# Late Q and K loads in rows of 2 KB, and one late store cut by partitions, in a cross-covariance attention kernel

## The chip, the cores and the metric

The kernel runs on one core of a Trainium2 chip. The metric is the device time of one execution in microseconds; of several executions the median is taken.

## The reference

Q, K and V have the shape (8, 12, 512, 64) in float32: 96 heads, 512 rows, 64 columns. Attention is taken between columns, not rows:

```python
Q_norm = Q / (norm(Q, axis=-2) + 1e-10)          # each column of 512 rows
K_norm = K / (norm(K, axis=-2) + 1e-10)
attn = einsum('bhnd,bhne->bhde', Q_norm, K_norm)  # 64 x 64 a head
attn = softmax(attn, axis=-1)
return einsum('bhnd,bhde->bhne', V, attn)
```

Q, K and V are 12.6 MB each, and so is the output: 50.3 MB have to pass between DRAM and the core.

## The kernel before, in words

The heads are taken four at a time: a **unit** u, 24 of them (`U`). Two units make a **step** s with halves r = 0 and 1 (u = 2s + r; 12 steps, `S`), and two steps share one V tile pair w (6 of them). In DRAM the units lie in the order w, r, e, where s = 2w + e.

For a unit, Q and K are loaded by `load_qk` with 16 rows of a head on a partition: 32 partitions a head, 4 KB in one piece for each partition. `cast_qk` writes them beside each other as bf16 (DVE). `grams` multiplies [Q K] by itself on TensorE, 32 partitions at a time: 16 products for each of four heads, 64 products a unit, each one a weight load and a matmul. The diagonal of the result gives the norms (`squares`, `sums`, `powers`), one quarter is Q times K (`cross`), which is scaled (`scale_k`), transposed (`logits`), exponentiated (`exps`) and normalised (`normalise`). V is loaded in rows of 8 KB (`load_v`), cast (`cast_v`, POOL or DVE), transposed on TensorE (`vtrans`, copied by `vcopy`), multiplied by the attention (`outs`, line 318), copied to the tile `so` (`ocopy`, ACT or DVE), and stored by `store`, two stores of 512 KB a step, 24 in all, with 2 KB in one piece.

All loads but two leave from SP's queue (the two first K loads leave from ACT), and so do all stores. The trace shows eight DMA semaphores in turn for this queue: a DMA is issued when the one eight places ahead has landed on all engines. In what follows this is called a lane.

The order of everything is made ahead of time by the class `Order`: each step of work is a piece with costs, what it must wait for, and a rank; a planner runs through them and emits the instructions in the order of its own times. Loads have the rank `QK_PACE * u / U` (lines 382 to 390) and `v_at`, stores that of V later by `ST_LAG`. `size` tells the planner how many TensorE instructions a piece has, because the planner models the fetching of TensorE's instructions in chunks of 256 (`pause`).

Some names that the change touches: `WIDE` is the first unit whose Q and K are loaded in another shape, with 8 rows of a head on a partition (64 partitions a head, two pieces of 2 KB for each partition, `Qw` and `Kw`), whose grams then take 64 partitions and 8 products a head. Before, `WIDE` is `U`, so no unit is of that kind. `parts(s)` says which steps load their two units by separate DMAs of 512 KB; the others load both by one DMA of 1 MB. `FEW = (S - 3, 1)` is one late store, the second of step 9; before, it leaves in four parts: partitions 0 to 91, 92 to 95 and 96 to 127 of its first half r = 0, and all 128 of its second half.

Of the kernel before, what the change touches and what calls it, by code (L numbers as in the profile page):

```python
# [102 lines left out]
def kernel(  # L103
# [7 lines left out]
    nc = tc.nc  # L111
    B, H, N, _ = Q.shape
    assert N == 32 * T and Q.shape[3] == D
    U = B * H // HU
    S = U // 2
    W = S // 2
    TAIL = 2
    WIDE = U
    ONE = 3
    HELD, UNTIL = ("lk", 1, 1), ("cq", 0, 1)  # L120
    BOTH = S - 8
# [10 lines left out]
    Qw = Q.rearrange("b h (p j) d -> (b h p j d)", j=J).rearrange("(u m p x) -> u p m x", m=2, p=128, x=J * D)  # L132
    Kw = K.rearrange("b h (p j) d -> (b h p j d)", j=J).rearrange("(u m p x) -> u p m x", m=2, p=128, x=J * D)
# [28 lines left out]
    qk32, v32, vb, qkb, gram, scr, kq, n2, r8, kqs, rq, lg, ex, ab, vps, vt, po, so = ({} for _ in range(18))  # L162
# [9 lines left out]
    def load_qk(s, x, r):  # L172

        w, e = divmod(s, 2)
        if s not in qk32:
            qk32[s] = qp.tile([128, 2, 2, T, D], F32, name="qk32")
        if HELD == ("l" + "qk"[x], s, r):

            nc.vector.memset(qk32[s][0:1, x, r, 0, 0:1], 0.0)
        if (s, x) == (0, 1):  # L180
            nc.scalar.dma_start(out=qk32[s][:, x, r].rearrange("p t d -> p (t d)"), in_=Ku[w, e, :, r])
        elif 2 * s + (r or 0) >= WIDE:
            nc.sync.dma_start(out=qk32[s][:, x, r].rearrange("p (m j) d -> p m (j d)", m=2), in_=(Qw, Kw)[x][U - 1])
        elif r is None:
            nc.sync.dma_start(out=qk32[s][:, x].rearrange("p r t d -> p r (t d)"), in_=(Qu, Ku)[x][w, e])  # L185
        else:
            nc.sync.dma_start(out=qk32[s][:, x, r].rearrange("p t d -> p (t d)"), in_=(Qu, Ku)[x][w, e, :, r])
# [10 lines left out]
    def store(s, i):  # L198
        o = Of[s // 2, s % 2, i].rearrange("p r (j d) -> p r j d", d=D)
        if (s, i) == FEW:  # L200

            for a, b in ((0, 92), (92, 96), (96, 128)):
                nc.sync.dma_start(out=o[a:b, 0], in_=so[s, i][a:b, 0])
            nc.sync.dma_start(out=o[:, 1], in_=so[s, i][:, 1])
            return
        nc.sync.dma_start(out=o, in_=so[s, i])

# [12 lines left out]
    def grams(u):  # L220
# [3 lines left out]
        if r == 0:  # L224
            gram[s] = ps_g.tile([128, HU, 2, 2, 2 * D], F32, name="gram")
        for t in range(T if u < WIDE else J):
            for h in range(HU):
                if u < WIDE:
                    x = qkb[u][32 * h:32 * (h + 1), t, :]
                else:  # L230
                    x = qkb[u][64 * (h % 2):64 * (h % 2 + 1), J * (h // 2) + t, :]
                nc.tensor.matmul(gram[s][:, h, r, 0], x, x, start=(t == 0), stop=(t == (T if u < WIDE else J) - 1))  # L232

# [96 lines left out]
    for r in range(2):  # L330
        load_qk(0, 0, r)
        load_qk(0, 1, r)
# [14 lines left out]
    for i in range(NB["ab"]):  # L347
        a = const.tile([128, HU, 2 * D], BF16, name=f"ab{i}")
# [3 lines left out]
    def size(key):  # L352
        if key[0] == "gr" and key[1] >= WIDE:
            return 64
        return 8 if key[0] == "vt" and key[-1] is not None else {"gr": 128, "lg": 8, "vt": 16, "ou": 16}[key[0]]
# [18 lines left out]


    def parts(s):
        return (0, 1) if s < ONE or s == S - 1 else (None,)

    def loaded(x, s, r):
        return ("l" + "qk"[x], s, r if len(parts(s)) == 2 else None)  # L380

    last = None
    for s in range(S):
        free = [back("cq", 2 * s + r, 2 * NB["qk"], x) for r in range(2) for x in range(2)]
        for r in parts(s):
            at = QK_PACE * (2 * s + (r or 0)) / U
            for x in range(2):
                key = loaded(x, s, r)
                piece(key, {"DMA": X if r is not None else 2 * X}, free, [last], at, load_qk, s, x, r)
                last = key  # L390
    for u in range(U):
        s, r = divmod(u, 2)
# [48 lines left out]
    for s in range(S):  # L441
        for x in range(4):
            i, k = divmod(x, 2)
            n = 4 * s + x - 2
            wait = [("oc", n // 4, n % 4)] if n >= 0 else []
            order = [("ou", s, x - 1) if x else back("ou", s, 1, 3)]
            piece(("ou", s, x), {"PE": 0.5}, [("vc", s // 2, *t) for t in turns(s // 2) if t[0] // 2 == k] + [("nm", s)] + wait, order, R["ou"] + 0.01 * s, outs, s, x)
            n = 2 * s + i - NB["so"]
            free = [("st", n // 2, n % 2)] if k == 0 and n >= 0 else []
            order = [("oc", s, x - 1) if x else back("oc", s, 1, 3)]  # L450
            piece(("oc", s, x), {"ACT": 0.6, "DVE": (0.68, BIAS["oc"])} if s >= BOTH else {"ACT": 0.6}, [("ou", s, x)] + free, order, R["oc"] + 0.01 * s, ocopy, s, x)
        for i in range(2):
            order = [("st", s, 0) if i else back("st", s, 1, 1)]
            piece(("st", s, i), {"DMA": X}, [("oc", s, 2 * i), ("oc", s, 2 * i + 1)], order, v_at(2 * s + i) + ST_LAG, store, s, i)
# [43 lines left out]
```

## Time and profile before

| | |
|---|---|
| median of 3 runs | 129.41 us (129.15 to 129.7) |
| span of the profiled execution | 127.4 us, 4949 instructions |
| profiled execution's own time | given as its span alone; the median lies 2.0 us above it |
| PE, PEld, DVE, ACT, POOL busy | 77.0, 62.7, 92.9, 72.3, 37.0 us |
| PE instructions | 2160 matmuls and 2160 weight loads |
| DMA | 14958 packets, 50.66 MB, mean 398 GB/s |
| queue of SP (q1) | 14648 packets, 95.9% of 16 engines' span |
| queue q8, kind instruction | 17 packets, 0.28 MB, 0.8% |
| HBM | 395 GB/s over the span |

The span runs from the first to the last instruction of the profiled execution. The row of DMA digits on the page gives for 40 equal slices how busy the 16 DMA engines were on average, in tenths. Times below are counted from the start of the span. A **lag** in the text is how much later one of the 16 DMA engines finishes its share of a DMA than the foremost engine does; it is read from the landing events that the trace keeps for each DMA, one for each engine that took part.

### The profile page before, as it was taken

Reading aid. Unit: us, or ns where it says so; the run is one execution under the profiler, and the core shown is the slowest. Engines: PE = TensorE matmul, PEld = TensorE weight load, DVE = VectorE, ACT = ScalarE, POOL = GpSimd, SP = SyncE. Lnnn points to the kernel's source line nnn. Section 1 sums busy time; section 2 is a strip of 40 time slices with the busy share of each in tenths; the row PEclk is TensorE's granted clock in tenths of the full one; section 3 lists DMA queues with packets and bytes.
Section 4 is the critical chain, followed back from the end, with each engine's and each line's share of the span. In section 5 each row is a group of like instructions: output and inputs, shape, how many; then the busy total and the mean of one; then the engine's idle time right before and its main releaser. Section 6 shows DMA issues by size and latency. Waiting matters only on the chain.

```text
span 127.4 us, 4949 instructions
## 1 busy us (share of the span) xinstructions
PE 77.0 (60%) x2160; PEld 62.7 (49%) x2160; DVE 92.9 (73%) x142; ACT 72.3 (57%) x220; POOL 37.0 (29%) x39
## 2 busy tenths in 40 slices
PE   0065393994837679859475986777597729753000
PEld 0054372783636568647354674666386517541000
DVE  3344749949899899999974989998999499950000
ACT  4000441559877077886691897583848919996000
POOL 4006307300916903033077011303733160300000
PEclk9999999999985555999996799869959995999755
DMA  4999999999999999999999999999999999999991
GB/s 113 413 438 408 428 411 418 417 433 408 435 418 414 411 417 424 402 415 427 423 414 414 415 428 417 415 424 425 401 420 419 401 402 410 395 408 408 375 377 60
DMA packets 14958, 50.66 MB, mean 398 GB/s; under 512 B 1112, under 2 KB 1112, under 8 KB 13400
## 3 DMA queue, kind: packets, MB, share of 16 engines
q1 hardware_dynamic: 14648, 49.29, 95.9%
q10 hardware_dynamic: 288, 1.05, 2.1%
q8 instruction: 17, 0.28, 0.8%
q14 instruction: 5, 0.04, 0.1%
HBM read 37.75 MB, written 12.58 MB: 395 GB/s over the span
## 4 chain that ended last, share of the span: by engine, by line
DVE 36%; PE 21%; DMA 19%; issue 8%; ACT 5%; SPq 1%; DVEq 0%; ACTq 0%
DVE qkb L212 15%; DMA qk<-in_K_dram 14%; PE gram L232 12%; DVE scr L239 7%; DMA qk<-in_Q_dram 5%; DVE vt L168 4%; PE vps L301 4%; DVE ab L290 4%; PE po L318 3%; ACT so L166 3%; DVE n L251 2%; ACT ex L281 2%; DVE vb L168 2%; PE lg L275 1%; SPq L185 1%
## 5 line engine op out<-in xcount | busy, mean ns | idle before, releaser
L232 PE MATMUL gram<-qkb 32*128 32x128 bf16 x1536 | 36.7, 259 | 24.8 <-issue 8.5
L232 PEld LDWEIGHTS <-qkb 32*128 32x128 bf16 x1536 | 30.8, 116 | 29.7 <-issue 11.1
L212 DVE CAST qkb<-qk 128x1024 bf16<-128x1024 f32 x48 | 37.7, 810 | 9.6 <-DMA qk<-in_Q_dram 8.0
L170 POOL TENSOR_SCALAR vb<-v 128x1024 bf16<-128x1024 f32 x18 | 21.7, 1215 | 43.9 <-DMA v<-in_V_dram 39.0
L166 ACT COPY vt<-vps 128x1024 bf16<-128x1024 bf16 (+1 forms) x18 | 17.8, 986 | 18.8 <-PE vps L301 18.7
L166 ACT COPY so<-po 128x512 f32<-128x512 f32 x45 | 24.9, 593 | 6.1 <-PE po L318 5.8
L318 PE MATMUL po<-ab,vt 128*64 128x128 bf16 x384 | 19.1, 237 | 6.2 <-issue 2.6
L262 POOL TENSOR_TENSOR kqs<-kq,r 64x512 f32<-64x512 f32 x12 | 14.0, 1169 | 29.1 <-ACT r L258 16.2
L301 PE MATMUL vps<-identb,vb 128*128 128x128 bf16 x192 | 18.5, 253 | 4.8 <-POOL vb L170 3.5
L239 DVE SCALAR_TENSOR_TENSOR scr<-gram,eye 64x512 f32<-64x512 f32 x24 | 16.5, 687 | 4.9 <-PE gram L232 4.7
L318 PEld LDWEIGHTS <-vt 128*64 128x64 bf16 x384 | 13.4, 117 | 10.4 <-issue 5.7
L301 PEld LDWEIGHTS <-vb 128*128 128x128 bf16 x192 | 14.0, 113 | 7.9 <-POOL vb L170 4.2
L281 ACT ACTIVATE ex<-lg,rq 128x64 f32<-128x64 f32 x48 | 14.5, 322 | 2.7 <-PE lg L275 2.6
L166 ACT COPY kq<-gram 64x512 f32<-64x512 f32 x12 | 7.0, 582 | 13.2 <-DVE scr L239 12.9
L290 DVE TENSOR_TENSOR ab<-ex,rinv 64x256 bf16<-64x256 f32 x24 | 12.8, 534 | 0.6
L281 ACT ACTIVATION_READ_ACCUMULATOR ex<-lg,rq 128x1 f32 x48 | 10.2, 213 | 0.0
L168 DVE CAST vb<-v 128x1024 bf16<-128x1024 f32 x6 | 7.4, 1241 | 1.8 <-DMA v<-in_V_dram 1.7
L275 PE MATMUL lg<-eye,kqs 64*128 64x64 f32 x48 | 6.4, 259 | 3.2 <-issue 1.6
L251 DVE TENSOR_REDUCE n<-scr 128x8 f32<-128x512 f32 x12 | 8.1, 679 | 0.1
L168 DVE COPY vt<-vps 128x1024 bf16<-128x1024 bf16 (+1 forms) x8 | 8.0, 1022 | 0.2
L275 PEld LDWEIGHTS lg<-eye,kqs 64*128 64x128 f32 x48 | 4.5, 156 | 5.0 <-issue 2.5
L287 DVE RECIPROCAL rinv<-esum 128x4 f32<-128x4 f32 x12 | 2.0, 170 | 2.5 <-ACT ex L281 2.4
(17 smaller groups left out, 16.0 us busy)
## 6 DMA issues: line engine op xcount, KB each, us to landing
v<-in_V_dram SPq DMA_DIRECT2D x12, 1024.0 KB, 17.4
out_dram<-so SPq DMA_DIRECT2D x23, 512.0 KB, 11.2
qk<-in_Q_dram SPq DMA_DIRECT2D x8, 1024.0 KB, 16.8
qk<-in_K_dram SPq DMA_DIRECT2D x8, 1024.0 KB, 18.8
qk<-in_Q_dram SPq DMA_DIRECT2D x8, 512.0 KB, 11.9
qk<-in_K_dram SPq DMA_DIRECT2D x6, 512.0 KB, 12.6
qk<-in_K_dram ACTq DMA_DIRECT2D x2, 512.0 KB, 7.3
out_dram<-so SPq DMA_DIRECT2D x1, 256.0 KB, 7.2
```

The source lines that it names most:

```text
L166: nc.scalar.copy(o, i)
L168: nc.vector.tensor_copy(o, i)
L170: nc.gpsimd.tensor_scalar(out=o, in0=i, scalar1=1.0, scalar2=0.0, op0=ALU.mult, op1=ALU.add)
L212: nc.vector.tensor_copy(qkb[u][:, :, x * D:(x + 1) * D], qk32[s][:, x, r])
L232: nc.tensor.matmul(gram[s][:, h, r, 0], x, x, start=(t == 0), stop=(t == (T if u < WIDE else J) - 1))
L239: nc.vector.scalar_tensor_tensor(out=scr[s][half], in0=gram[s][half, :, :, 0, half].rearrange("p h r d -> p (h r) d"), scalar=1e-20, in1=e ...
L262: (nc.vector if eng == "DVE" else nc.gpsimd).tensor_tensor(out=kqs[s][HI], in0=kq[s][HI], in1=r8[s][HI, :, None].to_broadcast([D, 2 * HU, ...
L275: nc.tensor.transpose(l[:, h, :], kqs[s][HI, 2 * h:2 * h + 2].rearrange("p r d -> p (r d)"), eye2[HI])
L281: nc.scalar.activation(e[:, h, :], lg[s][:, h, :], AF.Exp, scale=rq[s][:, h:h + 1], accum_out=z[:, h:h + 1])
L290: nc.vector.tensor_tensor(out=a[half, :, half], in0=e[half], in1=ri[half, :, None].to_broadcast([D, HU, D]), op=ALU.mult,)
L301: nc.tensor.transpose(ps[:, c, n, :], vb[w][:, J * c + j].rearrange("p r d -> p (r d)"), identb)
L318: nc.tensor.matmul(po[s, x][e * D:(e + 1) * D, j].rearrange("p r d -> p (r d)"), v, ab[s][:, h, :])
```

## The change

Three lines move. `WIDE` becomes `U - 3`, so that Q and K of units 21, 22 and 23 come in pieces of 2 KB, and their grams take 32 products instead of 64 each. `parts` lets step 10 load its two units by separate DMAs, as step 11 does already, since its second unit is now of the other shape. The late store leaves in two parts, 119 and 9 partitions, each with both halves.

```diff
-    WIDE = U
+    WIDE = U - 3
...
-            nc.sync.dma_start(out=qk32[s][:, x, r].rearrange("p (m j) d -> p m (j d)", m=2), in_=(Qw, Kw)[x][U - 1])
+            nc.sync.dma_start(out=qk32[s][:, x, r].rearrange("p (m j) d -> p m (j d)", m=2), in_=(Qw, Kw)[x][2 * s + r])
...
-            for a, b in ((0, 92), (92, 96), (96, 128)):
-                nc.sync.dma_start(out=o[a:b, 0], in_=so[s, i][a:b, 0])
-            nc.sync.dma_start(out=o[:, 1], in_=so[s, i][:, 1])
+            for a, b in ((0, 119), (119, 128)):
+                nc.sync.dma_start(out=o[a:b], in_=so[s, i][a:b])
...
-        return (0, 1) if s < ONE or s == S - 1 else (None,)
+        return (0, 1) if s < ONE or s >= S - 2 else (None,)
```

`Qw` and `Kw` count units in the order of DRAM and are indexed here by 2s + r, so units 21 and 22 read Q and K of each other's four heads; the amount and shape of what is moved and computed does not depend on that.

## The prediction

> **What bounds the kernel now.** I read the page first, its slices and its DMA rows.
>
> ```profile
> DMA  4999999999999999999999999999999999999991
> ...
> DMA packets 14958, 50.66 MB, mean 398 GB/s; under 512 B 1112, under 2 KB 1112, under 8 KB 13400
> ...
> q1 hardware_dynamic: 14648, 49.29, 95.9%
> ...
> q8 instruction: 17, 0.28, 0.8%
> ```
>
> From the second slice to the last but one the 16 DMA engines are full; no compute engine is (DVE leads with 73%). So the chain of waits, which gives DVE 36% and PE 21%, is not what I follow: work that only makes compute shorter has nothing to win while transfers queue. The end is a matter of which DMA engine is empty last, so I cut the tail into windows.
>
> ```profile
> 123.00:124.00 1.00, 0.00 (x0) 0.00 (x0) 0.00 (x0) 0.00 (x0) 0.00 (x0) 0.50 0.90 346
> 124.00:124.50 0.50, 0.00 (x0) 0.00 (x0) 0.00 (x0) 0.00 (x0) 0.00 (x0) 0.50 0.68 266
> 124.50:125.00 0.50, 0.00 (x0) 0.00 (x0) 0.00 (x0) 0.00 (x0) 0.00 (x0) 0.50 0.49 188
> 125.00:125.25 0.25, 0.00 (x0) 0.00 (x0) 0.00 (x0) 0.00 (x0) 0.00 (x0) 0.50 0.11 41
> 125.25:125.50 0.25, 0.00 (x0) 0.00 (x0) 0.00 (x0) 0.00 (x0) 0.00 (x0) 0.50 0.06 25
> 125.50:126.00 0.50, 0.00 (x0) 0.00 (x0) 0.00 (x0) 0.00 (x0) 0.00 (x0) 0.50 0.06 25
> 126.30:127.40 1.10, 0.00 (x0) 0.00 (x0) 0.00 (x0) 0.00 (x0) 0.00 (x0) 0.50 0.00 0
> ```
>
> The last two columns are DMA share and GB/s. A share of 0.06 is one engine of 16: from 125.2 to 126.2 us a single engine works alone, at 25 GB/s. Its last share lands at 126.53, and 0.90 us of waiting and closing follow to the span's end at 127.43. Why this one is late, the DMA answer for 117.5 to 127.4 us shows, and SP's timeline shows what is queued:
>
> ```profile
> q1 hardware_dynamic: 1448, 2.73, 71.6%
> q8 instruction: 1, 0.02, 0.6%
> ```
>
> ```profile
> 109.22 0.68 SPq L206 DMA_DIRECT2D out_dram<-so  x1
> 111.44 1.93 SPq L203 DMA_DIRECT2D out_dram<-so  x3
> 114.30 0.37 SPq L204 DMA_DIRECT2D out_dram<-so  x1
> 115.63 5.50 SPq L206 DMA_DIRECT2D out_dram<-so  x4
> ```
>
> One 16 KB instruction packet falls into the tail (trace: start 117.65, 960 ns). The late store is the four parts at L203 and L204; four stores follow it.
>
> **The model of the tail.** Landing events of the store issued at 109.22, the last before the parts: the foremost engine at 116.39, the others behind it by (us) 0.07, 0.15, 0.47, 0.47, 0.84, 1.23, 2.09, then seven by 2.77 to 3.02 and one by 4.29. Following the events back, the eight late ones rise in jumps of about 1.4 us, one jump an instruction packet: 17 packets, two on each of eight engines and the last, at 117.65, a third on one. The 92-row and the 4-row part land on four engines each, in the same pattern (118.31, 118.70, 119.08, 119.47 and 0.18 later). The packet count agrees: 71 issues with one 4-byte packet an engine would be 1136; the page has 1112, and 24 = 2 x 12. Taking back 23 rows from those times, the four have lags of 0.07, 0.46, 0.84 and 1.23.
>
> A store is 16 rows an engine and takes 1.278 us, 0.080 us a row. Engines of the four have 23 + 1 + 2 + 8 = 34 rows of the late store, the other twelve 2 + 8 = 10, and all have 64 rows of the four stores behind. The worst of the four: 116.39 + 1.23 + 98 x 0.080 + 0.04 (small packets) = 125.50; the trace has 125.50. The seven late ones: 116.39 + 3.02 + 74 x 0.080 + 0.03 = 125.36; trace 125.44 and less. The last: 116.39 + 4.29 + 5.94 = 126.62; trace 126.53. The model holds to 0.1 us.
>
> **The change, part by part.**
>
> *Fewer products.* Three units lose 32 products of two instructions: 4320 - 192 = 4128. Of TensorE's gaps of over 1.2 us, those before instructions 1982, 2238, 2494, 3006, 3262 and 4030 all lie at 190 plus a multiple of 256; the largest, 3.44 us before one matmul and charged to "issue", is at 4030. The next such edge, 4286, lies 34 before the end and asked for the packet at 117.65. With 4128 it is never reached: 16 packets, two for each of the eight. The last engine falls back by its jump, from 126.53 to where the next ones stand, 125.50: a gain of 1.03 us, if nothing else moved. The Trainium skill, in "Runtime: NRT & Kernel Launch", section "Instruction fetch mechanics", says that an engine's program comes in 16 KiB blocks of 256 instructions and that crossing a block is "mostly hidden". The block size agrees (17 packets of 16 KB); "hidden" does not hold here, where one packet sets back an engine by 1.5 us, and by that rule alone this edit would bring nothing.
>
> The matmuls saved (64 take 1.07 us when dense; 32 of twice the rows 0.5 to 1.1) are hidden: the last copy to `so` ends at 116.62, and the last two stores wait until 119.72 and 120.75 only for lanes. Afterwards those lanes are free by 116.85 (two parts instead of four), the last store goes when its copy is done, near 117, and the first engine wants it near 122.7. That cover is over 4 us; beyond it, each us of compute is a us.
>
> *2 KB rows.* Six DMAs of 512 KB: on each engine 48 packets of 4 KB become 96 of 2 KB. Step from packet to packet: 8 KB 307 ns (V loads), 4 KB 155 (Q, K), 2 KB 80 (stores). These fit one line, 75 a 2 KB and 5 a packet, so a 2 KB load should be 80: 48 x (160 - 155) = 0.24 us on all engines. Ends: nothing (halving 155), and 48 x 155 = 7.4 us if a packet's price didn't depend on its size, which 307 against 155 excludes; a load at 100 ns would be 2.2. I take 0.24; no other work hides it, since the engines are full.
>
> *Step 10 in two parts.* Two more issues on SP (0.35 us each), which otherwise waits for lanes (0.02 to 0.1 us after each landing here), and four issues of the store become two: the queue's count is as before. Ranks: units 20 and 21 are due at 0.526 and 0.552, V's next load at 0.537; that V load left long before (64.17, ahead of the pair at 66.48 and 68.47), so I expect the same order. Eight lanes of 512 KB at 1.28 us each are 10 us in flight. Cost 0.01 us, or up to 1 us if the planner lets a store that waits for its copy stand ahead of a load.
>
> *The store in 119 and 9.* 92, 4, 32 and 128 rows went to 4, 4, 16 and 16 engines: the largest number up to 16 that divides them. So 119 = 7 x 17 goes to seven engines, 34 rows of 2 KB each, and 9 to nine with 2 rows each: seven engines 36, two 2, seven none. The Trainium skill ("DMA: Bandwidth & Descriptors", "Why a DMA increments its semaphore by 16 and not by 1") states this rule, and that the lowest-numbered engines are taken; 92 and 4 here agree with it, and that the four are the lowest no row shows.
>
> The four keep their lags and get 2 rows more: the worst ends at 125.50 + 0.16 + 0.24 = 125.90. The three new ones: I take them from the engines without instruction packets, since those packets keep to a fixed eight and none of them is among the four; with lags up to 0.47 they end by 116.39 + 0.47 + 100 x 0.080 + 0.28 = 125.14. The eight end by 116.39 + 3.02 + 0.24 + 66 x 0.080 + 0.03 = 124.96. Last landing 125.90 against 126.53: -0.63 us. By parts: fetch -1.03, rows of the store +0.16, small packets +0.24. Profiled span 126.8; the median stands 1.98 above the span, and I carry the difference over: **128.8**.
>
> **Rivals.**
> (a) *Seven engines too many.* If one of the three new engines has a lag above 1.87 (126.53 - 116.39 - 8.03 - 0.24), the end moves back. The one at 2.09: +0.22, 129.6. One of the eight with instruction packets, 3.02: +1.15, **130.6**, slower. For it: I have the membership only by inference, and the engine of 2.09 is a neighbour. Against: the packets avoid the four.
> (b) *The last packet stays* (fetches not tied to the count) or its jump has another cause: then that engine keeps 4.29, but has no rows of the late store: 116.39 + 4.29 + 0.24 + 5.14 = 126.07, -0.46, 128.95. The forecast hardly hangs on the fetch. "Hidden", the Trainium skill's word for a block edge ("Runtime: NRT & Kernel Launch", "Instruction fetch mechanics"), would lead here.
> (c) *Lags of the seven are smaller* in plain runs, or fall on other engines: bounded by the eight at 124.96, -1.6, 127.8; half of that is 128.3.
> (d) *2 KB loads at 100 ns*: +1.9 over the forecast, 130.7.
> (e) *The planner's new order* leaves the queue empty for 1.5 us: 130.3. For: ranks and sizes change. Against: ten us in flight.
> (f) *119 rows on one engine*, if only powers of two count (92 and 4 can't tell): 220 rows more on one engine, some 17 us, 146. Against: all four counts seen are the largest whole divisor, and none needs the narrower rule. The section of the Trainium skill named for this store gives 10 engines for 100 partitions, which is not a power of two either; no run here shows that.
>
> **How the numbers follow.** About 0.5% (0.65 us) is what a measurement of this kernel can tell from no change; the forecast lies on that bound. Chances: forecast 0.50, of which I count 0.37 as faster, because the two rows and the packets are charged in full to the worst engine, and 0.13 as within; (c) 0.13, faster; (b) 0.04 and (a) at 2.09 0.03, within; (a) at 3.02 0.14, (d) 0.06, (e) 0.07, (f) 0.03, slower. Faster 0.50, within 0.20, slower 0.30. The forecast's own range is 128.2 to 129.2; with (a), (c) and (e) 127.9 to 130.7, with (a) whole; left out are (d), (f), and the ends of (c) and (a).
>
> **What would show it.** Right: 16 packets on q8, none after the last TensorE work; 2 KB load packets at a step of 80 ns; the tail of the DMA share ending with a few engines near 125.9; 7 and 9 landing events for the two parts. Wrong: a block of engines busy together past 126.5 (a), a DMA share under 0.9 before 120 (e), or a 119-row part that lands tens of us late (f).

## The result: slower by 0.75%, by rival (a), and the profile after

The changed kernel takes 130.33 us (median of 6 runs, 130.11 to 130.49) against 129.43 us before (6 runs, 129.05 to 129.7): ratio 1.0075, 95% interval 1.0059 to 1.0091. The forecast was 128.8. The span of the profiled execution grew from 127.4 to 128.5 us. These are the lines of its page that answer to those shown of before:

```profile
span 128.5 us, 4756 instructions
...
DMA  3999999999999999999999999999999999999971
...
DMA packets 15733, 50.64 MB, mean 394 GB/s; under 512 B 1120, under 2 KB 1120, under 8 KB 14176
...
q1 hardware_dynamic: 15424, 49.29, 95.4%
...
q8 instruction: 16, 0.26, 0.7%
```

Half of the forecast stands here: 16 instruction packets instead of 17, and the engines are full until the tail. The last slice but one, 9 before, is now 7, so the tail is thinner and longer. The windows of the tail (last two columns: DMA share, GB/s):

```profile
123.00:124.00 1.00, 0.00 (x0) 0.00 (x0) 0.00 (x0) 0.00 (x0) 0.00 (x0) 0.50 0.86 334
124.00:125.00 1.00, 0.00 (x0) 0.00 (x0) 0.00 (x0) 0.00 (x0) 0.00 (x0) 0.50 0.54 209
125.00:125.50 0.50, 0.00 (x0) 0.00 (x0) 0.00 (x0) 0.00 (x0) 0.00 (x0) 0.50 0.28 111
125.50:126.00 0.50, 0.00 (x0) 0.00 (x0) 0.00 (x0) 0.00 (x0) 0.00 (x0) 0.50 0.23 90
126.00:126.50 0.50, 0.00 (x0) 0.00 (x0) 0.00 (x0) 0.00 (x0) 0.00 (x0) 0.50 0.14 53
126.50:127.00 0.50, 0.00 (x0) 0.00 (x0) 0.00 (x0) 0.00 (x0) 0.00 (x0) 0.50 0.13 49
127.00:127.40 0.40, 0.00 (x0) 0.00 (x0) 0.00 (x0) 0.00 (x0) 0.00 (x0) 0.50 0.03 10
```

A share of 0.13 is two engines of 16: by the landing events of the last store (the third last at 126.42 us, then 127.37 and 127.56) two engines work alone for about 1 us, where before it was one. No instruction packet falls near: the DMA answer for 116 to 128.5 us names one queue only.

```profile
q1 hardware_dynamic: 1798, 3.45, 71.7%
```

The landing events say what these two are. The store before the cut one lands from 116.64 us on, the lags being 0.09, 0.11, 0.49, 0.55, 0.86, 1.42, 1.89 and then eight from 2.74 to 3.04. The 119-row part has seven landing events, at 119.49, 119.89, 120.24, 120.79, 121.21, 122.09 and 122.26. Taking back 34 rows of 0.080 us, the seven engines had lags of 0.13, 0.53, 0.87, 1.42, 1.85, 2.72 and 2.89: two of them are among the eight that carry instruction packets, for only those eight have lags above 2.7. (The trace does not name a packet's engine; the link is the jump in lag. The 16th packet starts at 114.03 us: one engine's lag is 1.45 in the store that it lands then and 2.80 in the next.) And the 9-row part's nine events begin at 116.86 and 116.91, so the eighth and ninth engine are among the foremost. The last of the seven should end at 116.64 + 2.89 + 100 x 0.080 + 0.03 = 127.56 us; the last store landed at 127.56.

SP's timeline shows that the order of issues is not to blame: all four last stores were issued by 118.5 us, nine before the last landing.

```profile
110.98 3.06 SPq L203 DMA_DIRECT2D out_dram<-so  x2
114.14 4.33 SPq L205 DMA_DIRECT2D out_dram<-so  x4
```

### The profile page after: what moved, and what is told of

It is laid out like the page before. It is cut to its first block, busy times and chain, and to the rows that moved or that the text cites. A ratio compares the mean times of both kernels' runs of the same rounds, so it can differ in the third digit from the quotient of the medians.

```text
span 128.5 us, 4756 instructions
## 1 busy us (share of the span) xinstructions
PE 79.8 (62%) x2064; PEld 65.3 (51%) x2064; DVE 91.6 (71%) x142; ACT 71.3 (55%) x219; POOL 36.5 (28%) x40
## 4 chain that ended last, share of the span: by engine, by line
DMA 42%; PE 15%; issue 12%; DVE 12%; ACT 6%; SPq 2%; POOL 1%; POOLq 1%; DVEq 0%
DMA qk<-in_Q_dram 23%; DMA out_dram<-so 10%; DMA qk<-in_K_dram 10%; PE gram L231 9%; DVE qkb L211 5%; PE po L317 5%; ACT so L166 4%; DVE scr L238 3%; SPq L194 1%; DVE vb L168 1%; POOL kqs L261 1%; ACT ex L280 1%; DVE so L168 1%; DVE n L250 1%; POOLq L492 1%
## 5 line engine op out<-in xcount | busy, mean ns | idle before, releaser
L231 PE MATMUL gram<-qkb 32*128 32x128 bf16 (+1 forms) x1440 | 37.7, 268 | 21.1 <-DVE qkb L211 7.8
L231 PEld LDWEIGHTS <-qkb 32*128 32x128 bf16 (+1 forms) x1440 | 32.0, 120 | 25.7 <-DVE qkb L211 9.5
L211 DVE CAST qkb<-qk 128x1024 bf16<-128x1024 f32 x48 | 35.1, 758 | 8.0 <-DMA qk<-in_Q_dram 6.1
L317 PE MATMUL po<-ab,vt 128*64 128x128 bf16 x384 | 21.8, 258 | 5.6 <-issue 2.2
L166 ACT COPY vt<-vps 128x1024 bf16<-128x1024 bf16 (+1 forms) x17 | 16.7, 984 | 15.2 <-PE vps L300 15.2
L317 PEld LDWEIGHTS <-vt 128*64 128x64 bf16 x384 | 15.8, 131 | 10.3 <-issue 7.1
L289 DVE TENSOR_TENSOR ab<-ex,rinv 64x256 bf16<-64x256 f32 x24 | 14.3, 595 | 0.6
L168 DVE COPY vt<-vps 128x1024 bf16<-128x1024 bf16 (+1 forms) x9 | 9.1, 1043 | 0.6 <-PE vps L300 0.5
L168 DVE CAST vb<-v 128x1024 bf16<-128x1024 f32 x5 | 6.1, 1225 | 0.7 <-DMA v<-in_V_dram 0.6
L256 ACT ACTIVATE ln<-n 128x8 f32<-128x8 f32 x12 | 2.7, 224 | 2.6 <-DVE n L250 2.6
```

The source lines that it names most:

```text
L166: nc.scalar.copy(o, i)
L168: nc.vector.tensor_copy(o, i)
L211: nc.vector.tensor_copy(qkb[u][:, :, x * D:(x + 1) * D], qk32[s][:, x, r])
L289: nc.vector.tensor_tensor(out=a[half, :, half], in0=e[half], in1=ri[half, :, None].to_broadcast([D, HU, D]), op=ALU.mult,)
L317: nc.tensor.matmul(po[s, x][e * D:(e + 1) * D, j].rearrange("p r d -> p (r d)"), v, ab[s][:, h, :])
```

## The experiments

Theory A: each engine's end is its lag plus its rows, and the change is slower because the 119-row part reaches two late engines. Theory B: 2 KB loads or products over 64 partitions cost the time. Theory C: the planner's new order does.

**The change without its store** (rows_only):

```diff
-            for a, b in ((0, 119), (119, 128)):
-                nc.sync.dma_start(out=o[a:b], in_=so[s, i][a:b])
+            for a, b in ((0, 92), (92, 96), (96, 128)):
+                nc.sync.dma_start(out=o[a:b, 0], in_=so[s, i][a:b, 0])
+            nc.sync.dma_start(out=o[:, 1], in_=so[s, i][:, 1])
```

> The change without its store: units 21 to 23 in 2 KB rows with 32 products, the late store in the four parts of before. Theory A (each DMA engine's end is its lag plus its rows; the change is slower because two of the seven engines of the 119-row part carry instruction packets): the 17th packet is gone, -1.03 us, small packets +0.24, the worst of the four engines ends near 125.7 to 126.0: median 128.6 to 128.9, faster by 0.4 to 0.6%. Theory B (2 KB loads, or products over 64 partitions, cost the time): 130.3 or more. Theory C (the planner's new order costs it): 130.3 too, with a DMA share under 0.95 somewhere before 118 us.

Measured: 128.71 us, ratio to before 0.9947 (0.9934 to 0.996). Theories B and C fall for the change as a whole: with all its loads, products and planning kept, the kernel is faster than before. The last landing is at 125.82, as A has it. The windows end early:

```profile
125.00:125.50 0.50, 0.00 (x0) 0.00 (x0) 0.00 (x0) 0.00 (x0) 0.00 (x0) 0.50 0.32 119
125.50:126.00 0.50, 0.00 (x0) 0.00 (x0) 0.00 (x0) 0.00 (x0) 0.00 (x0) 0.50 0.00 0
```

**The store alone** (store_only): the kernel before, with the cut of the change.

```diff
-            for a, b in ((0, 92), (92, 96), (96, 128)):
-                nc.sync.dma_start(out=o[a:b, 0], in_=so[s, i][a:b, 0])
-            nc.sync.dma_start(out=o[:, 1], in_=so[s, i][:, 1])
+            for a, b in ((0, 119), (119, 128)):
+                nc.sync.dma_start(out=o[a:b], in_=so[s, i][a:b])
```

> The store of 119 and 9 rows alone, all units in 4 KB rows with 64 products. Theory A: the engines of the seven with two instruction packets (lag 2.9) end at 116.39 + 2.9 + 8.0 = 127.3 us instead of 126.53: median 130.2; if the engine with the third packet is one of the seven, its lag of 4.3 gives 128.7 and a median of 131.6. Theories B and C: no slower than before, 128.9 to 129.4.

Measured: 130.13 us, ratio 1.0081 (1.0049 to 1.0113). Four of the six runs took 130.00 to 130.15, two 131.15 and 131.31. In the profiled one the engine with the third packet (lag 4.66) is not one of the seven (their lags by the same reckoning: 0.26 to 2.89). The two long runs are near the 131.6 that A gives if it is one of them, but they left no landing events to show it.

```profile
126.00:126.50 0.50, 0.00 (x0) 0.00 (x0) 0.00 (x0) 0.00 (x0) 0.00 (x0) 0.50 0.13 49
126.50:127.00 0.50, 0.00 (x0) 0.00 (x0) 0.00 (x0) 0.00 (x0) 0.00 (x0) 0.50 0.09 33
```

Again two engines at the end. The parts do not add up (-0.66 and +0.76 us, together +0.90), since the end is a largest value, not a sum: beside 17 packets the cut store also relieves the engine with the third packet, which ended last before (126.53 us) and here lands its last share by 126.3, and that relief is worth nothing once the third packet is gone.

**One unit only** (one_unit):

```diff
-    WIDE = U
+    WIDE = U - 1
```

> Only unit 23 in 2 KB rows with 32 products, the late store as before: 4256 TensorE instructions, still under the edge at 4286. Theory A: 16 instruction packets, -1.03 us, small packets +0.08: median 128.4 to 128.6, faster by 0.6 to 0.8%. Theory B: 129.4 plus a third of its cost, 129.7 or more. If the last packet does not set the end: 129.4 to 129.5.

Measured: 128.40 us, ratio 0.9926 (0.9914 to 0.9938): the lowest median of all versions, and faster than both kernels. 64 instructions fewer are enough to stay below the edge at 4286, for a third of the small packets. Unit 23 has the same number in both orders of units, so this version loads the same heads as the kernel before; the exchange of units 21 and 22 is in the change and in the versions made from it.

```profile
q8 instruction: 16, 0.26, 0.7%
```

**2 KB rows with the old number of instructions** (rows_64): rows_only, each product of the three units made twice.

```diff
-        for t in range(T if u < WIDE else J):
+        for t in list(range(T)) if u < WIDE else 2 * list(range(J)):
...
-        if key[0] == "gr" and key[1] >= WIDE:
-            return 64
```

> 2 KB rows for units 21 to 23 and the store of before, but each product of these units is made twice (the second pass overwrites the first), so that TensorE again has 4320 instructions and asks for 17 packets. Theory A: small packets alone, +0.24 us over before: 129.65; the difference from rows_only is what the 17th packet costs, 0.8 to 1.0 us. Theory B (2 KB loads): as slow as the change, 130.3. If the count of packets does not matter, equal to rows_only.

Measured: 129.69 us, ratio 1.0019 (1.0009 to 1.003). The lone engine at the end is back, and the 17th packet with it:

```profile
125.50:126.00 0.50, 0.00 (x0) 0.00 (x0) 0.00 (x0) 0.00 (x0) 0.00 (x0) 0.50 0.06 25
126.00:126.50 0.50, 0.00 (x0) 0.00 (x0) 0.00 (x0) 0.00 (x0) 0.00 (x0) 0.50 0.06 25
```

```profile
q8 instruction: 17, 0.28, 0.8%
```

By the medians, one instruction packet costs 129.69 - 128.71 = 0.98 us here. The twelve runs of rows_64 fall into two groups, five at 129.39 to 129.43 us and seven at 129.68 to 129.94, so it is 0.7 us in some executions and 1.1 in others; why, no run shows. The 2 KB rows of three units cost 0.2% of before, 0.25 us (by the interval 0.1 to 0.4).

**Which engine is late** (map_before, map_after): the first half of the late store in parts that land on the first 5, 6, 7, 9, 10, 11 and more engines.

```diff
-            for a, b in ((0, 92), (92, 96), (96, 128)):
-                nc.sync.dma_start(out=o[a:b, 0], in_=so[s, i][a:b, 0])
+            c = 0
+            for n in (5, 6, 7, 9, 10, 11, 12, 13, 14, 15, 26):
+                nc.sync.dma_start(out=o[c:c + n, 0], in_=so[s, i][c:c + n, 0])
+                c += n
             nc.sync.dma_start(out=o[:, 1], in_=so[s, i][:, 1])
```

> The kernel before, with the first half of the late store in parts of 5, 6, 7, 9, 10, 11, 12, 13, 14, 15 and 26 partitions: a part of n lands on n engines, one row each, so each part's landing events give the lags of the first n engines, and the difference between two parts the lag of each further engine. Theory A: the first seven include two of the eight late engines (lags 2.6 to 3.0 us) and the one near 1.9 to 2.1; the eighth and ninth are at 0 to 0.15; of the last seven, six are late. A rival, that the seven engines of the change were slow because the 119-row part leaves in another way than a plain store: lags of the first seven all under 2.1 here. The time is not of interest: 17 small parts pass eight lanes.

> The changed kernel with the same eleven parts in place of 119 and 9. Theory A: the same engines are late as in map_before, with 16 packets and none at 4.3 us. If membership changes from kernel to kernel, another set of engines is late, and the change was slow by chance.

The store leaves in 12 parts here (not 17, as the expectation says); each version ran once, 131.18 and 131.51 us, with before at 129.29. Landing events of the first parts, in us (from the trace; each part takes about 0.18 us more on every engine that it meets):

```
map_before
 5 rows  116.85 117.02 117.50 118.06 119.12
 6 rows  117.03 117.19 117.68 118.24 119.31 119.40
 7 rows  117.21 117.37 117.86 118.43 119.33 119.50 119.61
 9 rows  116.70 116.70 117.38 117.54 118.04 118.60 119.53 119.70 119.82
map_after
 5 rows  116.95 117.26 117.68 118.24 118.86
 6 rows  117.13 117.43 117.86 118.42 119.04 119.78
 7 rows  117.30 117.60 118.03 118.59 119.23 119.71 119.98
 9 rows  116.89 116.99 117.49 117.78 118.22 118.77 119.42 119.92 120.18
```

Each longer part keeps the events of the shorter one and adds new ones, so the sets are nested. In both kernels the first four engines rise to a lag of about 1.4, the fifth is at 2.0 to 2.4, the sixth and seventh are late (2.6 to 2.9), the eighth and ninth are the foremost of all. The 10-row and the 11-row part of map_before add an event at 119.73 and one at 119.60: the tenth and eleventh are late. From the twelfth on the parts are issued too late to tell. Eight late engines less these four leave four late ones among the last five (balanced, below, says more). As far as the parts tell, the late set is the same in both kernels, so it is no chance of one program; a rival in which the 119-row part is slow by its kind falls, since parts of 6 and 7 rows meet the same late engines.

**Half of the cut** (half_seven): the changed kernel, only the store's first half in 119 and 9.

```diff
-                nc.sync.dma_start(out=o[a:b], in_=so[s, i][a:b])
+                nc.sync.dma_start(out=o[a:b, 0], in_=so[s, i][a:b, 0])
+            nc.sync.dma_start(out=o[:, 1], in_=so[s, i][:, 1])
```

> The changed kernel, but only the first half of the late store leaves in 119 and 9 partitions; the second half leaves whole, on 16 engines. The seven engines then have 17 + 1 + 8 = 26 rows of the store instead of 36. Theory A: the late pair among the seven ends 10 x 0.080 = 0.8 us sooner: 129.5. If splitting by 119 has a price of its own, whatever the rows: 130.3, or half of the loss against rows_only, 129.5 as well only by chance; if only the whole store suffers, 128.7.

Measured: 129.38 us, ratio 0.9989 (0.9979 to 1.0). Ten rows fewer on the seven bring the ratio down from 1.0075 by 0.86% of before, 1.1 us, where the rows give 0.8; the trace's last landing, 126.55, is 1.01 us earlier than the change's. The 0.2 us beyond the rows lie in where the engines stood: the foremost engine landed the store ahead at 116.56 instead of 116.64 us, and the worst of the seven had a lag of 2.77 instead of 2.89. This time alone does not tell A from a price of its own. The change's trace does: with 34 rows taken back, the lags of the seven are those of the store ahead to within 0.05 us, and lag and rows give the last landing without such a price.

**The uneven store earlier** (early):

```diff
-    FEW = (S - 3, 1)
+    FEW = (S - 5, 1)
```

> The changed kernel with the cut store two steps earlier (the second of step 7 instead of step 9). Theory A: what counts is each engine's sum of work, not the place of the uneven store: 130.2 to 130.4, the change's time. A rival, that an uneven store is only harmful where little is queued behind it: 128.7 to 129.0.

Measured: 130.21 us, ratio 1.0058 (1.0042 to 1.0074): as the change, whose interval (1.0059 to 1.0091) overlaps. A heavy share is not made good by what is queued behind it, because everything behind it is shared evenly.

**A more even cut** (balanced): one_unit with

```diff
-            for a, b in ((0, 92), (92, 96), (96, 128)):
+            for a, b in ((0, 76), (76, 128)):
```

> One unit in 2 KB rows, as in one_unit, with the first half of the late store in parts of 76 and 52 partitions: 19 rows on each of four engines, 4 on each of 13, then 8 on all for the second half. Theory A: the fourth engine (lag 1.5) has 31 rows instead of 34 and ends 0.24 us sooner, the late ones 12 instead of 10 or 11: the last end comes 0.15 us sooner than in one_unit, 128.2 to 128.3. Without it, 128.4 as one_unit.

Measured: 128.58 us, ratio 0.9921 (0.9904 to 0.9939), against one_unit's 0.9926 (0.9914 to 0.9938). The two are not told apart; 0.15 us is below what these runs resolve. But the 52-row part, with 13 landing events, says more of the late engines than the map could. Two of its events are at 116.92 and 116.97 us (the eighth and ninth engine), then none before 118.58. Seven lie at 119.61 to 120.05: one is the fourth engine's, which had landed its 19 rows at 119.42, and the other six have lags of 2.7 to 3.1. So the twelfth and the thirteenth engine are late too, and of the last three two are late and one is not.

## Why the prediction was wrong

The model was right and one assignment in it was wrong: "The three new ones: I take them from the engines without instruction packets". They were given lags up to 0.47; in the changed kernel the fifth engine has 1.85, and the sixth and seventh have 2.72 and 2.89. The reason given, that the packets keep to a fixed eight and avoid the four, holds, but does not make the eight the last ones in order. The sixth and seventh engine belong to them, the eighth and ninth don't, and the fifth is slow without being one of them. Rival (a) named this and its price: 130.6 us for a lag of 3.02. The measured 130.33 is that with a lag of 2.89 (0.13 less) and a median that stands 1.9 instead of 2.0 us above the span.

- **Fetch, -1.03 us:** right. 16 packets; 0.98 us between rows_64 and rows_only, and one_unit's 0.97 us below before. In the kernel before, TensorE passed instruction 4286 at 114.65 us and ended its last product at 116.0, before the 17th packet started at 117.65: no work waited for this packet, but it took its place in an engine's queue. The Trainium skill calls the crossing of a block "mostly hidden" ("Runtime: NRT & Kernel Launch", "Instruction fetch mechanics"). For TensorE's work at this edge that is so; for the time of this kernel, whose DMA engines are full, it is not.
- **2 KB rows, +0.24 us:** right. The foremost engine reached the cut store at 116.64 instead of 116.39, and four consecutive 2 KB loads of 512 KB follow each other by 1.28 to 1.29 us, 0.080 us a row; before, the last four loads of 512 KB, in pieces of 4 KB, did so by 1.24 to 1.26. Rival (d) falls.
- **The store, +0.16 us:** the term that failed. It costs about 130.33 - 128.71 = 1.62 us (before stood at 129.43 beside the one and 129.37 beside the other); the last landings, 127.56 and 125.82, lie 1.74 apart. The prediction let the worst of the four end last, at 125.90, and rows_only does end near that, at 125.82; in the changed kernel the last to end is one of the three added. The count of engines was right: 7 and 9 landing events, as the largest divisor gives. Rival (f) falls. "DMA: Bandwidth & Descriptors" of the Trainium skill ("Why a DMA increments its semaphore by 16 and not by 1") states this rule and that the lowest-numbered engines are taken. The nested parts agree with that, though no row here names an engine.
- **Compute hidden:** right. The last copy to `so` ended at 116.21 us, and the issue of the last store began at 117.19, 3.8 us before the foremost engine landed the store ahead of it. The 96 products over 64 partitions take 252 ns each by the page's groups, about what the narrow ones take (269), at half the number.
- **Order:** nearly as expected; two stores that left ahead of step 11's loads now leave behind the last V load. The DMA share stays full, so rival (e) falls; rows_only has the same loads and gains.

Whoever means to load the first seven engines has to know the fifth, sixth and seventh. No DMA of the kernel before tells engines apart beyond the first four, so its profile could not show them; a run such as map_before could have, ahead of the change. The chance of 0.14 that I gave it came from a guess about order; three engines drawn blindly from the twelve others, of which eight are late, would have met a late one nearly always.

## What to carry to other kernels

Where all DMA engines are full, the time is set by the engine that ends last, its lag and its rows together, so read the tail by engines: a DMA share of 1/16 at the end is one engine's extra, and its landing events say how much. A change that moves work between engines needs to know which engines are late, not how many; a store cut into parts of 5, 6, 7 and 9 rows measures that in one run. And counting instructions against the next block of 256 can be worth more than making them faster: 64 fewer of 4320 brought 0.7%.

## What the runs showed of the hardware that was not expected

- An instruction packet of 16 KB takes 0.93 us on its engine (mean of the 17 before, 0.88 to 0.97), but sets it back by about 1.4 us against the others, twice on each of the same eight engines.
- Those eight are not in a row: the sixth, the seventh, the tenth to the thirteenth and two of the last three in the order in which a DMA on few engines takes them.
- One engine, by its lag the fifth, falls behind by about 0.08 us a store between 104 and 116 us, in both kernels, and stops about when compute ends (before, its lag grows from 1.33 to 2.07 us and then stays). What it does there no run shows.
